# Choosing experts on ScalarE and VectorE: where the gate factors, the number lookup and the first-key rows are computed

## The chip, the core and the metric

One Trainium2 chip, one of its NeuronCores. The metric is the device time of one execution of the whole kernel, in microseconds (us); the number quoted for a kernel is the median of its runs. The engines are named as the profile names them: PE (TensorE, matrix products), DVE (VectorE), ACT (ScalarE), POOL (GpSimd) and SP (SyncE, which only issues transfers here). POOL also issues the gathers of expert rows.

## What is computed

One layer on 1024 tokens of 1024 values: a mixer of two groups (state space and convolution), then retrieval of experts, then a norm. The change lies in the retrieval. Cut to what matters:

```
s = einsum("thpd,hpkd->thpk", q, sub_keys)          # 8 heads, 2 halves, 128 keys each
sv, si = top_k(s, 16)                               # best 16 of 128 keys, both halves
cand = sv[:, :, 0, :, None] + sv[:, :, 1, None, :]
best, flat = top_k(cand.reshape(t, 8, 256), 16)     # best 16 of the pair sums
i1 = take(si[:, :, 0], flat // 16); i2 = take(si[:, :, 1], flat % 16)
experts = i1 * 128 + i2                             # 128 numbers out of 16384 for a token
gates = softmax(best)
act = gelu(einsum("pd,ped->pe", x, u_tab[experts]))
out = einsum("pe,ped->pd", gates * act, v_tab[experts])
```

## The kernel before, in words

Tokens come in eight blocks of 128 (z = 0 to 7). Blocks 0 to 4 are served densely: for every expert the product with all tokens is made, weighted by a gate matrix that is zero for experts that a token didn't choose. Blocks 5 to 7 are served by gathers: POOL issues indirect transfers of single expert rows, and DVE multiplies and adds them. Both kinds run side by side in the last stage (from about 1246 us to the end), where PE does the dense products.

Before that comes the stage of choice (some 717 to 1211 us). `select` (L1016) chooses the experts of a block. For each head DVE finds the best 16 of the 128 scores of each half (`top16`, L1024). POOL adds the pairs of key numbers (`stair` on POOL, L1056) and DVE adds the pairs of scores (L1057); then DVE finds the best 16 of 50 candidate sums. The number lookup follows: for each head, two one-hot arrays are made by comparison on DVE (L1081; 128x160 for the first eight places, 128x400 for the others), multiplied in place by the candidate numbers on POOL (L1083), and summed on DVE one head later (`place`, L1069). Then come the softmax (L1089 to L1097, its exponential on ACT) and the next block. `select` is a generator; each yield carries an estimated time.

For blocks 0 to 4, `gate_matrix` (L1166) writes the gate matrices to DRAM (`g_dram`). It takes four tokens (index t4) at a time, 32 times a block, 160 times in all:

- `second` (L1200): DVE compares the second key numbers with 0 to 127 and gets one-hot rows `ob` in bfloat16, laid out key by token (L1203). POOL multiplies them by the gates and writes `o2` token by key (L1205).
- `first` (L1208): one-hot rows `o1` of the first key number. Three times out of four DVE compares (L1211); the fourth time ACT computes relu(1 - |key - number|) in four activations of one token and one over all four (L1216, L1217).
- `outer` (L1186): PE multiplies `o2` by `o1` for each of the four tokens into one PSUM tile `pg` (L1189).
- `store` (L1192): ACT copies `pg` into a staging tile `stg` (L1196), laid out row, column, token. After every 16 of these SP writes the tile to `g_dram` (L1198).

One step of `gate_matrix` works on four groups at once: it stores group n-3, makes the second rows of n, the first rows of n-1 and the product of n-2 (L1222 to L1226). Buffers: 3 for `ob`, 4 for `o2`, 2 for `o1`, 3 for `pg`.

The order of work is written out: every engine carries out its instructions in the order in which the program issues them. While `select` runs for a block, `tick` (L1118) adds up the estimated times and issues one step of the waiting gate matrix for each 1.0 us, and one piece of the score products (L947, `scores`) for each 1.75 us. So the gate matrix of block z is woven into the choice for block z+1. At the end of the stage `prepare` (L994) makes the first dense products; it splits operands on DVE and POOL in turn (L1002, L61).

Block 7 is chosen inside the last stage: `choosing` (L1340) calls the same `select`, two heads at a time, and `advance` (L1347) issues one of its pieces after each group of dense products, and a step of `gathered` (L1272) where it is due. There POOL's queue holds both the lookup's products (L1083) with the sums of key numbers (L1035), and the gathers (L1281), in one order. A gather waits for one of five row buffers, which DVE frees by L1303 or L1315. PE's dense products use expert matrices that ACT and DVE split into a high and a low part (`lower_u`, L982; `hi_lo`, L61).

The places that the change touches:

Of the kernel before, what the change touches and what calls it, by code (L numbers as in the profile page):

```python
# [13 lines left out]
AF = mybir.ActivationFunctionType  # L14
OP = mybir.AluOpType
# [3 lines left out]
P = 128  # L19
# [53 lines left out]
def layer_kernel(ctx, tc, A, dbg=None):  # L73
    nc = tc.nc
# [10 lines left out]
    ones = glob.tile([P, P], F32, name="ones")  # L85
    nc.vector.memset(ones, 1.0)
    iot = glob.tile([P, P], F32, name="iot")
# [85 lines left out]
    with ExitStack() as st:  # L173
# [80 lines left out]
        for i in range(NZ):  # L254
            o = prb[:, i * P:(i + 1) * P] if i < NT else prc[:, (i - NT) * P:(i - NT + 1) * P]
# [111 lines left out]
    with ExitStack() as st:  # L367
# [126 lines left out]
        for n, c in enumerate(order):  # L494
# [5 lines left out]
            p, pc = project(n, 4 <= c < 10 or c == 20)  # L500
# [7 lines left out]
            elif c >= 16 and c < 20:  # L508
                i = c - 16
# [18 lines left out]
            else:  # L528
                i = c - 4
# [241 lines left out]
    with ExitStack() as st:  # L771
# [129 lines left out]
        for z in range(NT):  # L901
# [3 lines left out]
            p = multiply(z, 0, x1)  # L905
# [8 lines left out]
            p = multiply(z, 1, x1)  # L914
# [101 lines left out]
    def select(z, tp, nh, scores, put):  # L1016

        def together(chains):
            for c in zip(*chains):
                for f in c:  # L1020
                    f()
                yield len(c)
# [17 lines left out]
        for h0 in range(0, NH, nh):  # L1040

            v = tp.tile([P, nh, 2, TOPK], F32, name="v", bufs=1)
            ix = tp.tile([P, nh, 2, TOPK], U32, name="ix", bufs=1)
            for hh in range(nh // 2):
                s = scores(z, h0 // 2 + hh)
                for q in (0, 1):
                    for n in together([top16(v[:, 2 * hh + q, p], ix[:, 2 * hh + q, p], s[:, 2 * q + p],
                                             tp.tile([P, P], F32, name="scr", bufs=2)) for p in range(2)]):
                        yield 0.2 * n
            ixf = ix.bitcast(F32)  # L1050
            nc.vector.tensor_copy(ixf, ix)
            nc.vector.tensor_scalar(ixf[:, :, 0], ixf[:, :, 0], float(P), None, op0=OP.mult)
            yield 0.3

            cand = tp.tile([P, 2, nh, NCAND], F32, name="cand", bufs=1)
            stair(nc.gpsimd, ixf, cand[:, 1], UPPER + LOWER)  # L1056
            stair(nc.vector, v, cand[:, 0], SUMS)  # L1057
            yield 1.0
            best = tp.tile([P, nh, TOPK], F32, name="best", bufs=1)
            pos = tp.tile([P, nh, TOPK], U32, name="pos", bufs=1)  # L1060
            posf = tp.tile([P, nh, TOPK], F32, name="posf", bufs=1)
            ef, gt = put(z, h0)
            pend = []

            def place(n):
                while len(pend) > n:
                    q, oh = pend.pop(0)
                    for i, o in enumerate(oh):
                        nc.vector.tensor_reduce(ef[:, q, i * 8:i * 8 + 8], o, axis=mybir.AxisListType.X, op=OP.add)  # L1069

            for q2 in range(0, nh, 2):
                for n in together([top16(best[:, q], pos[:, q], cand[:, 0, q], tp.tile([P, NCAND], F32, name="c2", bufs=2))
                                   for q in (q2, q2 + 1)]):
                    yield 0.12 * n
                nc.vector.tensor_copy(posf[:, q2:q2 + 2], pos[:, q2:q2 + 2])
                for q in (q2, q2 + 1):
                    oh = tp.tile([P, 8, NUP + NCAND], F32, name="oh").rearrange("p a b -> p (a b)")
                    oh = [o.rearrange("p (a b) -> p a b", a=8) for o in (oh[:, :8 * NUP], oh[:, 8 * NUP:])]
                    for i, o in enumerate(oh):
                        sh = [P, 8, NCAND if i else NUP]  # L1080
                        nc.vector.tensor_tensor(o, posf[:, q, i * 8:i * 8 + 8, None].to_broadcast(sh),  # L1081
                                                lex[:, None, :sh[2]].to_broadcast(sh), op=OP.is_equal)
                        nc.gpsimd.tensor_tensor(o, o, cand[:, 1, q, None, :sh[2]].to_broadcast(sh), op=OP.mult)  # L1083
                    pend.append((q, oh))
                    yield 0.7
                    place(nh // 8)
                    yield 0.7
            eb = tp.tile([P, nh, TOPK], F32, name="eb", bufs=1)
            nc.vector.tensor_tensor(eb, best, best[:, :, 0:1].to_broadcast([P, nh, TOPK]), op=OP.subtract)  # L1089
            nc.scalar.activation(eb, eb, AF.Exp)  # L1090
            yield 0.2
            place(0)
            yield 0.9
            sm = tp.tile([P, nh], F32, name="sm")
            nc.vector.tensor_reduce(sm, eb, axis=mybir.AxisListType.X, op=OP.add)
            nc.vector.reciprocal(sm, sm)
            nc.vector.tensor_tensor(gt, eb, sm[:, :, None].to_broadcast([P, nh, TOPK]), op=OP.mult)  # L1097
            if z >= ND:
                nc.vector.tensor_copy(idx[:, z - ND, h0 * TOPK:(h0 + nh) * TOPK], ef.rearrange("p h k -> p (h k)"))
            yield 0.8  # L1100
# [5 lines left out]
    with ExitStack() as st:  # L1106
# [59 lines left out]
        def gate_matrix(z, ef, gt):  # L1166

            e2 = tp2.tile([P, 2, P], F32, name="e2", bufs=1)
            ei = e2[:, 0].bitcast(I32)
            nc.vector.tensor_copy(ei, ef)  # L1170
            nc.vector.tensor_scalar(ei, ei, P - 1, None, op0=OP.bitwise_and)
            nc.vector.tensor_copy(e2[:, 1], ei)
            nc.vector.tensor_tensor(e2[:, 0], ef, e2[:, 1], op=OP.subtract)
            nc.vector.tensor_scalar(e2[:, 0], e2[:, 0], 1.0 / P, None, op0=OP.mult)
            yield
            pt = psT.tile([P, 3, P], F32, name="pt")
            for j, src in enumerate((e2[:, 0], gt, e2[:, 1])):
                nc.tensor.transpose(pt[:, j], src, ident)
            tr = tp2.tile([P, 2, P], F32, name="tr", bufs=1)
            tb = tp2.tile([P, P], BF16, name="tb", bufs=1)  # L1180
            yield
            nc.scalar.activation(tr, pt[:, :2], AF.Copy)
            nc.scalar.activation(tb, pt[:, 2], AF.Copy)
            yield

            def outer(t4, o1, o2):  # L1186
                pg = psG.tile([P, 4, P], F32, name="pg")
                for j in range(4):
                    nc.tensor.matmul(pg[:, j], o2[:, j], o1[:, j], start=True, stop=True)  # L1189
                return t4, pg  # L1190

            def store(t4, pg):  # L1192
                if t4 % 16 == 0:
                    stg[0] = gst.tile([P, P, P // 2], F32, name="stg")
                o = t4 % 16 * 4
                nc.scalar.activation(stg[0][:, :, o:o + 4].rearrange("p i t -> p t i"), pg, AF.Copy)  # L1196
                if t4 % 16 == 15:
                    nc.sync.dma_start(g_dram[z, t4 // 16], stg[0])  # L1198

            def second(t4):  # L1200
                ts = slice(t4 * 4, t4 * 4 + 4)
                ob = tp2.tile([P, P, 4], BF16, name="ob", bufs=3)
                nc.vector.tensor_tensor(ob, iotx, tb[:, None, ts].to_broadcast([P, P, 4]), op=OP.is_equal)  # L1203
                o2 = tp2.tile([P, 4, P], F32, name="o2", bufs=4)
                nc.gpsimd.tensor_tensor(o2.rearrange("p t j -> p j t"), ob, tr[:, 1, None, ts].to_broadcast([P, P, 4]), op=OP.mult)  # L1205
                return t4, o2

            def first(t4, o2):  # L1208
                o1 = tp2.tile([P, 4, P], F32, name="o1")
                if t4 % 4 < 3:  # L1210
                    nc.vector.tensor_tensor(o1, iot[:, None].to_broadcast([P, 4, P]),  # L1211
                                            tr[:, 0, t4 * 4:t4 * 4 + 4, None].to_broadcast([P, 4, P]), op=OP.is_equal)
                else:
                    for j in range(4):
                        t = t4 * 4 + j
                        nc.scalar.activation(o1[:, j], iot, AF.Abs, bias=tr[:, 0, t:t + 1], scale=-1.0)  # L1216
                    nc.scalar.activation(o1, o1, AF.Relu, bias=ones[:, 0:1], scale=-1.0)  # L1217
                return t4, o1, o2

            stg = [None]  # L1220
            got = [None] * 3
            for t4 in range(P // 4 + 3):  # L1222
                if got[2]:
                    store(*got[2])
                got = [second(t4) if t4 < P // 4 else None, got[0] and first(*got[0]), got[1] and outer(*got[1])]
                yield  # L1226
# [369 lines left out]
```

## Time and profile before

| | |
|---|---|
| time, median of 3 runs | 3130.14 us (3124.53 to 3130.31) |
| the profiled execution's own time | 3129.54 us |
| its span in the profile | 3127.7 us |
| PE, DVE, POOL, ACT busy over the span | 91%, 84%, 55%, 32% |

The span is what the profiler sees between the first and the last instruction; the execution's own time has 1.84 us around it. Busy shares are means over the span; the stages differ, so the prediction goes by stretches. Matrix products on PE are pipelined, and their ends are modelled.

### The profile page before, as it was taken

How to read it: one execution, taken by the hardware profiler on the slowest of the kernel's cores; microseconds unless marked ns; L12 is line 12 of the kernel's file. 1: busy time of each engine (PE TensorE's matmuls, PEld its weight loads, DVE VectorE, ACT ScalarE, POOL GpSimd, SP SyncE). 2: the span in 40 equal slices, each digit the busy share in tenths (PEclk: the TensorE clock that was granted, in tenths of full speed). 3: DMA queues.
4: the chain of work that ended last, by engine and by line, in shares of the span. 5: the costliest groups of instructions: out<-in, count | busy, mean ns of one | idle time of the engine just before them, and what ended most of it. 6: DMA issues, size and time to landing. Idle time of an engine off the chain costs nothing.

```text
span 3127.7 us, 41600 instructions
## 1 busy us (share of the span) xinstructions
PE 2841.5 (91%) x14905; PEld 2381.7 (76%) x14905; DVE 2632.5 (84%) x4956; ACT 1011.7 (32%) x1584; POOL 1713.4 (55%) x1361
## 2 busy tenths in 40 slices
PE   7999777998888875999989999999999999999996
PEld 3777676764555555887878988998998898898885
DVE  5898788559999997889888888888888888888886
ACT  3224323333555652232222222222222322222222
POOL 0221454425676774666666666565566555556663
PEclk8999999999999887999999999999999999999998
DMA  6111355250222125888879999999998998999983
GB/s 209 61 40 42 112 150 184 81 188 7 115 108 108 55 122 199 286 277 314 297 273 326 320 336 339 328 334 326 327 334 315 328 349 314 334 335 322 327 290 127
DMA packets 334543, 722.65 MB, mean 231 GB/s; under 512 B 24560, under 2 KB 167168, under 8 KB 333056
## 3 DMA queue, kind: packets, MB, share of 16 engines
q0 software_dynamic: 112176, 408.47, 36.8%
q1 hardware_dynamic: 222160, 311.53, 29.0%
q8 instruction: 117, 1.92, 0.2%
q14 instruction: 90, 0.74, 0.1%
HBM read 658.56 MB, written 61.35 MB: 230 GB/s over the span
## 4 chain that ended last, share of the span: by engine, by line
PE 44%; DVE 29%; issue 10%; DMA 8%; POOL 6%; ACT 2%; SPq 0%; DVEq 0%; POOLq 0%; ACTq 0%
PE pa L990 18%; PE pv L1428 5%; PE pv L1429 5%; PE pv L1427 5%; POOL gr L1281 4%; DMA gr<-in_peer_u_dram,idx 4%; DVE cfm L408 3%; DVE o L1211 3%; PE pa L68 3%; DVE ob L1203 2%; PE pq L947 2%; DVE oh L1081 2%; DMA gr<-in_peer_v_dram,idx 2%; DVE gr L1303 1%; DVE h2T L1315 1%
## 5 line engine op out<-in xcount | busy, mean ns | idle before, releaser
L1281 POOL DMA_INDIRECT gr<-in_peer_v_dram,idx x384 | 537.6, 1400 | 325.5 <-DVE h2T L1315 219.1
L1281 POOL DMA_INDIRECT gr<-in_peer_u_dram,idx x384 | 523.8, 1364 | 347.9 <-DVE gr L1303 262.5
L1428 PE MATMUL pv<-vl,wh 128*128 128x512 f32 x1280 | 513.4, 401 | 26.0 <-DVE vl L61 25.9
L1315 DVE SCALAR_TENSOR_TENSOR h2T<-gr,wv,h2T 128x1024 f32<-128x1024 f32 x381 | 495.7, 1301 | 38.3 <-DMA gr<-in_peer_v_dram,idx 31.5
L1427 PE MATMUL pv<-vh,wl 128*128 128x512 f32 x1280 | 510.6, 399 | 7.2 <-ACT vh L60 7.0
L1303 DVE SCALAR_TENSOR_TENSOR gr<-gr,h2T 128x1024 f32<-128x1024 f32 x384 | 463.9, 1235 | 57.5 <-DMA gr<-in_peer_u_dram,idx 52.8
L1429 PE MATMUL pv<-vh,wh 128*128 128x512 f32 x1280 | 510.7, 399 | 0.0
L60 ACT ACTIVATE vh<-v 128x512 fp32r<-128x512 f32 x256 | 161.8, 632 | 682.6 <-PE pv L1429 656.1
L990 PE MATMUL pa<-hh,ul 128*128 128x320 f32 x2000 | 340.3, 313 | 40.1 <-DVE ul L982 39.2
L990 PE MATMUL pa<-hl,uh 128*128 128x320 f32 x2000 | 336.8, 311 | 8.3 <-ACT uh L978 8.3
L990 PEld LDWEIGHTS pa<-hh,ul 128*128 128x128 f32 x2000 | 306.6, 190 | 45.4 <-DVE ul L982 44.4
L990 PE MATMUL pa<-hh,uh 128*128 128x320 f32 x2000 | 337.6, 311 | 0.0
L990 PEld LDWEIGHTS pa<-hl,uh 128*128 128x128 f32 x2000 | 307.8, 190 | 11.3 <-ACT uh L978 8.6
L1428 PEld LDWEIGHTS pv<-vl,wh 128*128 128x128 f32 x1280 | 243.2, 190 | 92.4 <-DVE vl L61 35.7
L990 PEld LDWEIGHTS pa<-hh,uh 128*128 128x128 f32 x2000 | 307.5, 190 | 0.0
L1392 ACT ACTIVATE ga<-pa 128x320 f32<-128x320 f32 x252 | 110.0, 438 | 594.7 <-PE pa L990 571.0
L1427 PEld LDWEIGHTS pv<-vh,wl 128*128 128x128 f32 x1280 | 243.6, 190 | 66.4 <-ACT vh L60 8.2
L1429 PEld LDWEIGHTS pv<-vh,wh 128*128 128x128 f32 x1280 | 243.4, 190 | 57.8
L1205 POOL TENSOR_TENSOR o<-ob,tr 128x512 f32<-128x512 bf16 x160 | 216.5, 1355 | 110.7 <-DVE ob L1203 99.4
L1189 PEld LDWEIGHTS pg<-o,o 128*128 128x128 f32 x1280 | 173.9, 207 | 132.5 <-issue 66.4
L61 DVE TENSOR_TENSOR vl<-v,vh 128x512 fp32r<-128x512 f32 x256 | 184.4, 721 | 105.1 <-ACT vh L60 104.1
L1189 PE MATMUL pg<-o,o 128*128 128x128 f32 x1280 | 187.4, 297 | 78.8 <-DVE o L1211 53.9
(357 smaller groups left out, 4510.3 us busy)
## 6 DMA issues: line engine op xcount, KB each, us to landing
v<-in_peer_v_dram SPq DMA_DIRECT2D x256, 256.0 KB
u<-in_peer_ut_dram SPq DMA_DIRECT2D x87, 512.0 KB
g_dram<-stg SPq DMA_DIRECT2D x10, 4096.0 KB
gm<-g_dram SPq DMA_DIRECT2D x64, 640.0 KB
h2T<-in_peer_ut_dram SPq DMA_DIRECT2D x41, 512.0 KB
ld<-in_ada_w_dram SPq DMA_DIRECT2D x24, 512.0 KB
w<-in_w_in_t_dram SPq DMA_DIRECT2D x21, 512.0 KB
raw<-in_ada_w_dram SPq DMA_DIRECT2D x8, 1024.0 KB
```

The lines of the kernel that those rows point to most:

```text
L60: nc.scalar.activation(hi, src, AF.Copy)
L61: (eng or nc.vector).tensor_tensor(lo, src, hi.bitcast(F32), op=OP.subtract)
L990: nc.tensor.matmul(pa[half], x[:, k], y[:, k, half * TH:half * TH + TH], start=t == 0 and k == 0, stop=t == 2 and k == KD - 1)
L1189: nc.tensor.matmul(pg[:, j], o2[:, j], o1[:, j], start=True, stop=True)
L1205: nc.gpsimd.tensor_tensor(o2.rearrange("p t j -> p j t"), ob, tr[:, 1, None, ts].to_broadcast([P, P, 4]), op=OP.mult)
L1281: nc.gpsimd.indirect_dma_start(out=g, out_offset=None, in_=A[t], in_offset=bass.IndirectOffsetOnAxis(ap=idx[:, b, e:e + 1], axis=0))
L1303: nc.vector.scalar_tensor_tensor(g, g, 1.0, h2, op0=OP.mult, op1=OP.mult, accum_out=act[:, e:e + 1])
L1315: nc.vector.scalar_tensor_tensor(ac, g, wv[:, e:e + 1], ac, op0=OP.mult, op1=OP.add)
L1392: nc.scalar.activation(self.ga[:, half * TH:half * TH + TH], self.pa[half], AF.Gelu)
L1427: nc.tensor.matmul(Out.pv[t], wl[:, sl], self.vh, start=i == 0, stop=False)
L1428: nc.tensor.matmul(Out.pv[t], wh[:, sl], self.vl, start=False, stop=False)
L1429: nc.tensor.matmul(Out.pv[t], wh[:, sl], self.vh, start=False, stop=i == GE - 1)
```

## The change

Four edits in `select` and `gate_matrix`. The products of the number lookup move from POOL to DVE. The eviction of the gate matrix writes in the staging tile's own order (row, then four tokens in a run) and reads the PSUM tile in steps, where before it read PSUM in order and wrote in steps. The multiplication of the second-key rows by the gates becomes four activations with a scale per partition on ACT, in place of one operation on POOL. All first-key rows are made by comparison on DVE; the form on ACT is gone.

```diff
--- before.py
+++ after.py
@@ -1080,7 +1080,7 @@
                         sh = [P, 8, NCAND if i else NUP]
                         nc.vector.tensor_tensor(o, posf[:, q, i * 8:i * 8 + 8, None].to_broadcast(sh),
                                                 lex[:, None, :sh[2]].to_broadcast(sh), op=OP.is_equal)
-                        nc.gpsimd.tensor_tensor(o, o, cand[:, 1, q, None, :sh[2]].to_broadcast(sh), op=OP.mult)
+                        nc.vector.tensor_tensor(o, o, cand[:, 1, q, None, :sh[2]].to_broadcast(sh), op=OP.mult)
                     pend.append((q, oh))
                     yield 0.7
                     place(nh // 8)
@@ -1193,7 +1193,7 @@
                 if t4 % 16 == 0:
                     stg[0] = gst.tile([P, P, P // 2], F32, name="stg")
                 o = t4 % 16 * 4
-                nc.scalar.activation(stg[0][:, :, o:o + 4].rearrange("p i t -> p t i"), pg, AF.Copy)
+                nc.scalar.activation(stg[0][:, :, o:o + 4], pg.rearrange("p t i -> p i t"), AF.Copy)
                 if t4 % 16 == 15:
                     nc.sync.dma_start(g_dram[z, t4 // 16], stg[0])
 
@@ -1202,19 +1202,14 @@
                 ob = tp2.tile([P, P, 4], BF16, name="ob", bufs=3)
                 nc.vector.tensor_tensor(ob, iotx, tb[:, None, ts].to_broadcast([P, P, 4]), op=OP.is_equal)
                 o2 = tp2.tile([P, 4, P], F32, name="o2", bufs=4)
-                nc.gpsimd.tensor_tensor(o2.rearrange("p t j -> p j t"), ob, tr[:, 1, None, ts].to_broadcast([P, P, 4]), op=OP.mult)
+                for j in range(4):
+                    nc.scalar.activation(o2[:, j], ob[:, :, j], AF.Copy, scale=tr[:, 1, t4 * 4 + j:t4 * 4 + j + 1])
                 return t4, o2
 
             def first(t4, o2):
                 o1 = tp2.tile([P, 4, P], F32, name="o1")
-                if t4 % 4 < 3:
-                    nc.vector.tensor_tensor(o1, iot[:, None].to_broadcast([P, 4, P]),
-                                            tr[:, 0, t4 * 4:t4 * 4 + 4, None].to_broadcast([P, 4, P]), op=OP.is_equal)
-                else:
-                    for j in range(4):
-                        t = t4 * 4 + j
-                        nc.scalar.activation(o1[:, j], iot, AF.Abs, bias=tr[:, 0, t:t + 1], scale=-1.0)
-                    nc.scalar.activation(o1, o1, AF.Relu, bias=ones[:, 0:1], scale=-1.0)
+                nc.vector.tensor_tensor(o1, iot[:, None].to_broadcast([P, 4, P]),
+                                        tr[:, 0, t4 * 4:t4 * 4 + 4, None].to_broadcast([P, 4, P]), op=OP.is_equal)
                 return t4, o1, o2
 
             stg = [None]
```

## Rows read from the trace of the kernel before

**Rows 1.** Stretches; columns: us, busy PE, PEld, DVE, ACT, POOL, granted clock, DMA share, GB/s.
```profile
748.00:1180.00 432.00, 353.17 (x1682) 240.67 (x1681) 424.80 (x1624) 248.96 (x399) 307.14 (x306) 0.93 0.22 93
1246.00:1650.00 404.00, 367.86 (x1952) 329.14 (x1953) 344.00 (x708) 111.73 (x176) 255.56 (x217) 0.95 0.84 290
1650.00:2050.00 400.00, 395.48 (x2172) 353.82 (x2172) 346.99 (x437) 110.35 (x175) 246.56 (x178) 1.00 0.94 329
```

**Rows 2.** Waits from 748 to 1180 us: total us, times, longest.
```profile
ACT stg L1196 <- PE pg L1189: 138.4, 96, 5.2
...
PE pg L1189 <- DVE o L1211: 53.9, 38, 4.2
```

**Rows 3.** DVE's groups by shape, 717 to 1211 us: busy us, mean ns | idle before.
```profile
L1211 DVE TENSOR_TENSOR o<-iot,tr 128x512 f32<-128x512 f32 x120 | 100.0, 834 | 1.7 <-PE pg L1189 1.6
L1203 DVE TENSOR_TENSOR ob<-iotx,tb 128x512 bf16<-128x512 bf16 x160 | 95.6, 598 | 0.0
L1081 DVE TENSOR_TENSOR oh<-posf,lex 128x400 f32<-128x400 f32 x56 | 43.4, 775 | 0.0
...
L1081 DVE TENSOR_TENSOR oh<-posf,lex 128x160 f32<-128x160 f32 x56 | 23.1, 412 | 1.4
...
L1075 DVE CAST posf<-pos 128x32 f32<-128x32 uint32 x28 | 11.5, 410 | 0.8
```

**Rows 4.** The same lines one by one: shortest/median/longest ns, first and last start.
```profile
L1203 DVE TENSOR_TENSOR ob<-iotx,tb x160: 397/474/1258, 748.6 to 1173.7; 128x512 bf16<-128x512 bf16 x160
...
L1211 DVE TENSOR_TENSOR o<-iot,tr x120: 675/684/1551, 750.7 to 1174.0; 128x512 f32<-128x512 f32 x120
...
L1081 DVE TENSOR_TENSOR oh<-posf,lex x128: 309/562/1898, 721.3 to 1611.1; 128x160 f32<-128x160 f32 x64, 128x400 f32<-128x400 f32 x64
...
L1075 DVE CAST posf<-pos x32: 175/240/1082, 721.1 to 1596.8; 128x32 f32<-128x32 uint32 x32
```

**Rows 5.** Timeline, one meeting of POOL and DVE: start us, us.
```profile
885.48 1.54 POOL L1205 TENSOR_TENSOR o<-ob,tr 128x512 f32<-128x512 bf16 x1 [0.36 <-PE pg L1189]
...
885.98 1.26 DVE L1203 TENSOR_TENSOR ob<-iotx,tb 128x512 bf16<-128x512 bf16 x1
```

**Rows 6.** Timeline of DVE: two that depend, a step's start, two that don't depend.
```profile
744.34 0.23 DVE L1171 TENSOR_SCALAR e<-e 128x128 int32<-128x128 int32 x1
744.61 0.23 DVE L1172 CAST e<-e 128x128 f32<-128x128 int32 x1
...
758.16 0.41 DVE L1203 TENSOR_TENSOR ob<-iotx,tb 128x512 bf16<-128x512 bf16 x1
...
765.99 0.41 DVE L1203 TENSOR_TENSOR ob<-iotx,tb 128x512 bf16<-128x512 bf16 x1
766.32 0.68 DVE L1211 TENSOR_TENSOR o<-iot,tr 128x512 f32<-128x512 f32 x1
```

**Rows 7.** ACT: two groups by shape, then two merged pieces of its timeline.
```profile
L1196 ACT ACTIVATE stg<-pg 128x512 f32<-128x512 f32 x159 | 166.3, 1063 | 143.9 <-PE pg L1189 138.4 <-POOL o L1205 5.3
...
L953 ACT ACTIVATE s<-pq 128x512 f32<-128x512 f32 x24 | 14.9, 619 | 6.8 <-PE pq L947 6.8
...
882.26 1.24 ACT L1216 ACTIVATE o<-iot,tr 128x128 f32<-128x128 f32 x4
...
885.47 1.98 ACT L1196 ACTIVATE stg<-pg 128x512 f32<-128x512 f32 x2 [1.21 <-PE pg L1189]
```

**Rows 8.** 1246 to 1650 us: a wait's total, then timeline pieces of PE and POOL.
```profile
POOL oh L1083 <- DVE oh L1081: 30.2, 7, 9.6
...
1323.96 0.50 PE L1427 MATMUL pv<-vh,wl 128*128 128x512 f32 x1 [1.95 <-ACT vh L60]
...
1391.47 2.50 PE L990 MATMUL pa<-hh,ul 128*128 128x320 f32 x8 [5.52 <-DVE ul L982]
...
1611.36 2.60 POOL L1083 TENSOR_TENSOR oh<-oh,cand 128x160 f32<-128x160 f32 x2 [5.60 <-DVE oh L1081]
...
1621.43 2.50 PE L990 MATMUL pa<-hh,ul 128*128 128x320 f32 x8 [7.26 <-DVE ul L982]
```

## The prediction, made before the changed kernel was run

> **What bounds the kernel now.** I read the page's shares first, and they don't decide: PE and DVE are both busy most of the span. So I went by stretches, then by waits, then by DVE's groups and the single durations in them.
>
> In the stage of choice DVE is busy 424.8 of 432 us, PE 353, POOL 307, ACT 249 [rows 1]. A busy share of 98% on an engine that works in order means that its own work sets the pace. The waits agree: PE waits 53.9 us for DVE's first-key rows and ACT waits 138.4 us for PE [rows 2], while DVE's comparisons wait 1.6 us for PE in all [rows 3].
>
> But DVE's busy time isn't all work. The same comparison of one shape takes 0.40 us at best and 1.26 us at worst for `ob`, 0.68 (median) and 1.55 for `o1` [rows 4]; the means are 0.60 and 0.83 [rows 3]. One meeting shows why: POOL multiplies from 885.48 to 887.02, and an `ob` comparison that starts at 885.98 ends at 887.24, as if it had run its 0.40 us only once POOL was done [rows 5]. So POOL's two products (L1205, L1083) cost DVE time, though POOL itself is no bound.
>
> In the last stage PE sets the pace, with an exception. From 1650 to 2050 us it is busy 395.5 of 400 at a granted clock of 1.00; from 1246 to 1650, while block 7 is chosen, 367.9 of 404 at 0.95 [rows 1]: some 36 us idle against 4.5. There POOL waits 30.2 us for DVE's comparisons, seven times [rows 8], and while it waits its queue issues no gather. DVE, in order, then waits for the late row, the split matrix behind it comes late, and PE waits for that. Of PE's gaps over 1 us, seven (the first 1.95 us at 1324, the last 7.26 us at 1621) come up to some 10 us after a lookup product on POOL, 20.8 us in all; the others, as the 5.52 us before 1391, follow the sums of key numbers, which stay on POOL [rows 8].
>
> **The stage of choice, on DVE.** Seven blocks are chosen in it: 56 heads and 160 groups of four tokens.
>
> What leaves DVE is the waiting for POOL. From the groups' busy time [rows 3] I take the count times the undisturbed duration [rows 4]: `ob` 95.6 - 160 x 0.40 = 31.6; `o1` 100.0 - 120 x 0.684 = 17.9; the one-hots, 43.4 - 56 x 0.56 = 12.0 and 23.1 - 56 x 0.31 = 5.7; the casts of positions 11.5 - 28 x 0.18 = 6.5. That is 73.7 us. On POOL only the sums of key numbers and four splits are left. Bounds: none of it goes (0), or all of it and some 6 us more in small groups that I don't list (80). I take 77, nearer the upper end, since the undisturbed durations stand in the same trace.
>
> What comes to DVE, first: 112 lookup products. They aren't in DVE's trace; the nearest row is the comparison of the same shapes and type, 0.31 and 0.56 us [rows 4]. Each needs the result just before it. Dependent operations start 0.03 us after the end of the one in front, independent ones 0.08 before it (766.32 against 765.99 + 0.41) [rows 6]. So a head's four operations take 0.34 + 0.23 + 0.59 + 0.48 = 1.64 us where two take 0.23 + 0.48 = 0.71: 56 x 0.93 = 52 us more. Bounds: 40 us if they overlap like independent ones, 60 if the candidates' repeated rows read slower.
>
> Second: 40 first-key rows, 40 x (0.68 - 0.08) = 24 us.
>
> DVE's sum is 52 + 24 - 77 = -1, with -16 (40 + 24 - 80) as its lower end and +7 (60 + 24 - 77) as its upper; that POOL stays in the way is the last rival below.
>
> **New waits.** The exponential (L1090) now stands on ACT behind an eviction and four gate activations, and DVE's sum (L1095) is queued behind its result: seven times at most 2.1 us, 0 to 15 us. I take 1, since DVE has the last lookup sums and a step of the gate matrix in between. The lookup's products now wait on DVE for POOL's sums of key numbers; the search for the best 16 covers these, and in the last stage several pieces of dense work do; without that cover it is a POOL wait of the kind seen at 1391. `ob` has three buffers, now freed by ACT, which works behind PE: three steps of slack, no cost while ACT keeps up. SP's queue gets the same ten transfers. So the stage comes to 0.
>
> **ACT.** Per group of four it now does one eviction, 0.97 us from start to start (two in 1.98), and four activations, 1.24 us together and 1.15 behind one another, if they take what its four of the same shape take now [rows 7]; those are gone. With 0.1 for the scores' evictions (14.9 us [rows 7] over 160) that is 2.2 us a group. DVE has 425 us / 160 = 2.66 us a group in the mean, but less in quick stretches, beside the search among the 128 scores: four steps from 758.16 to 765.99, 1.96 each [rows 6], and 2.1 with their share (0.60/4) of the extra rows. By the estimated times in the code (16 of a block's 35 us) about half of the steps, 80, are such. So ACT is under DVE where an eviction takes less than some 0.87 us from start to start.
>
> The eviction's new price isn't in the trace. From PSUM to SBUF in order, 128x512 takes 0.62 us; written in steps of 256 bytes, 1.06 [rows 7]. It now writes runs of four and reads PSUM in steps of 512 bytes, which no row shows. Bounds: 0.62, and 1.50 if stepped reading costs 0.44 us too and none of the stepped writing's 0.44 goes. I take 0.7 (0.61 from start to start), nearer the first, since the step that made the known difference is gone. Then ACT costs nothing; it is DVE's work that hides it.
>
> [...]
>
> **The last stage.** POOL no longer waits for comparisons, so gathers go out earlier. At best the 20.8 us of PE's gaps go, and some of the time at the lower clock with them; at worst none goes, because the gathers find the next holdup. I take 16, since the stair sums and the full buffers stay. DVE gets 8 heads x 0.93 = 7.4 us more; it is busy 344 of 404 us there [rows 1], so its pauses hide most of it; I charge 2. Net -14, ends -21 and +7. PE after 1650 us is untouched.
>
> **Sum**, against the profiled execution's 3129.5 us: 0 - 14, or **3115.5 us**. The median of the runs, 3130.1, stands 0.6 us above that execution, so this is 0.47% below it. What a measurement of this kernel can tell from no change is about 0.2%, some 6 us.
>
> **Rivals.**
>
> *The gathers stay late.* The stair sums and the full buffers hold POOL as long as the products did, and the stage of choice breaks even: 3130 us, no difference. For it: PE's gaps behind stair sums, that of 5.52 us among them. Against: the longest, 7.26 us, follows a lookup product for which POOL had waited 5.60 us [rows 8]. Chance 0.21.
>
> *ACT becomes the bound*, the slower end. Place: the gate steps beside the search among 128 scores, 748 to 1180 us. It decides from an eviction of 0.87 us start to start. Price: with 0.97, as now, 80 x (2.2 - 2.1) = 8 us; with 1.40 (1.50 less the overlap), 80 x (2.65 - 2.1) = 44. I take the middle, 26: 3115.5 + 26 = 3141.5 us. For it: no row has the stepped reading. Against: only stepped writing has a price in rows. [...] Chance 0.20.
>
> *POOL wasn't what stretched DVE's operations*, so the relief doesn't come: 3115.5 + 77 = 3192.5 us. Against: the meeting [rows 5], and undisturbed durations in the same stage [rows 4]. Chance 0.03.
>
> **Numbers.** My forecast has 0.56; its own range is 3097 to 3125, from -12 to +8 in the stage of choice and -21 to -12 in the last. For 8 in 10 the range also takes in no difference and the nearer part of the ACT case: 3095 to 3146. Faster by over 0.2%: 0.53 of the forecast, 0.03 of the late gathers, 0.03 of the ACT case. Within 0.2%: 0.03, 0.16 and 0.06 of the same. Slower: 0.02 of the late gathers, 0.11 of the ACT case and the 0.03 of the last.
>
> **What would show it.** Right: `ob` near 0.40 us and `o1` near 0.68 in the mean, lookup products near 0.31 and 0.56 on DVE, the stage of choice still ending near 1211 us with DVE over 95% busy, evictions near 0.7, fewer and shorter PE gaps from 1246 to 1650. Wrong: DVE idle behind ACT, PE waiting for the gate activations, evictions over 0.96 us (0.87 from start to start), or the same PE gaps behind late gathers.

## The result

The changed kernel takes 3115.52 us (median of 5 runs, 3108.79 to 3116.64) against 3130.14 us before (median of 5, 3124.53 to 3139.56); the ratio is 0.9945, with a 95% interval of 0.9925 to 0.9965. The forecast was 3115.5 us.

Three stretches of the profile after, in the columns of [rows 1]:

```profile
748.00:1180.00 432.00, 350.58 (x1674) 238.94 (x1675) 420.63 (x1778) 302.22 (x843) 16.79 (x56) 0.92 0.22 93
1246.00:1650.00 404.00, 377.86 (x2061) 340.90 (x2062) 358.52 (x741) 117.73 (x186) 250.84 (x208) 0.96 0.88 304
1650.00:2050.00 400.00, 395.71 (x2135) 351.01 (x2134) 345.63 (x446) 107.59 (x171) 242.17 (x179) 1.00 0.94 331
```

In the stage of choice POOL has gone from 307 us of work to 17, ACT from 249 to 302, and DVE is as full as before: 421 of 432 us. From 1246 to 1650 us PE does 10 us more work in the same time; after 1650 nothing differs.

DVE's groups in the stage of choice after (717 to 1260 us), which answer to [rows 3]; L1083 is the lookup product, now on DVE:

```profile
L1211 DVE TENSOR_TENSOR o<-iot,tr 128x512 f32<-128x512 f32 x160 | 109.8, 686 | 0.2 <-PE pg L1189 0.2
L1203 DVE TENSOR_TENSOR ob<-iotx,tb 128x512 bf16<-128x512 bf16 x160 | 66.4, 415 | 0.0
L1083 DVE TENSOR_TENSOR oh<-oh,cand 128x400 f32<-128x400 f32 x56 | 32.2, 575 | 2.4
L1081 DVE TENSOR_TENSOR oh<-posf,lex 128x400 f32<-128x400 f32 x56 | 31.8, 569 | 0.1
...
L1081 DVE TENSOR_TENSOR oh<-posf,lex 128x160 f32<-128x160 f32 x56 | 19.4, 347 | 1.4
L1083 DVE TENSOR_TENSOR oh<-oh,cand 128x160 f32<-128x160 f32 x56 | 19.4, 346 | 2.4
...
L1075 DVE CAST posf<-pos 128x32 f32<-128x32 uint32 x28 | 5.9, 212 | 0.8
```

The means of the comparisons have come down to what was their undisturbed duration before: 0.415 from 0.598 us for `ob`, 0.686 from 0.834 for `o1`. The products cost what comparisons of their shapes do.

ACT's two new groups (L1206 is the gate multiplication), which answer to [rows 7], and the scores' eviction (L953), which reads PSUM and writes SBUF in order, for comparison:

```profile
L1206 ACT ACTIVATE o<-ob,tr 128x128 f32<-128x128 bf16 x640 | 209.4, 399 | 92.4 <-DVE ob L1203 90.4
L1196 ACT ACTIVATE stg<-pg 128x512 f32<-128x512 f32 x160 | 92.8, 580 | 16.4 <-PE pg L1189 16.3
L953 ACT ACTIVATE s<-pq 128x512 f32<-128x512 f32 x29 | 16.9, 583 | 25.6 <-PE pq L947 25.6
```

The eviction fell from 1.063 to 0.580 us, as fast as the one that does both in order (0.583).

**Where the time went.** Three events mark the stages in every kernel: the first score product (L947), the first product with a gathered row of the first table (L1303, after the change L1298), and the first multiply-add with one of the second table (L1315, then L1310). In the rows by line, the first of the two times is the first start. Before:

```profile
L947 PE MATMUL pq<-m,h2T x512: 592/592/1222, 681.0 to 1153.7; 128*128 128x512 f32 x171
...
L1303 DVE SCALAR_TENSOR_TENSOR gr<-gr,h2T x384: 1199/1218/2540, 1241.0 to 2753.8; 128x1024 f32<-128x1024 f32 x192
...
L1315 DVE SCALAR_TENSOR_TENSOR h2T<-gr,wv,h2T x381: 1265/1284/3433, 1569.7 to 3054.8; 128x1024 f32<-128x1024 f32 x191
```

After:

```profile
L947 PE MATMUL pq<-m,h2T x512: 592/592/1220, 686.1 to 1154.4; 128*128 128x512 f32 x171
...
L1298 DVE SCALAR_TENSOR_TENSOR gr<-gr,h2T x384: 1198/1221/1281, 1242.7 to 2739.1; 128x1024 f32<-128x1024 f32 x192
...
L1310 DVE SCALAR_TENSOR_TENSOR h2T<-gr,wv,h2T x381: 1267/1284/3436, 1556.6 to 3041.4; 128x1024 f32<-128x1024 f32 x191
```

The stage of choice, from the first to the second event, took 560.0 us and takes 556.6; the first table's part, in which most of block 7 is chosen, 328.7 and 313.9; the rest of the span 1558.0 and 1557.1. That is 19.1 us less. In the profiled execution after the change, the part ahead of the scores, which the change doesn't touch, came out 5.1 us longer, so the span shows 14.0. Such a later start (686 in place of 681 to 683 us) stands in two of the ten profiles below, so the stages are compared by their lengths:

| kernel | stage of choice | first table | rest | span | median | ratio to before (95%) |
|---|---|---|---|---|---|---|
| before | 560.0 | 328.7 | 1558.0 | 3127.7 | 3130.1 | |
| after | 556.6 | 313.9 | 1557.1 | 3113.7 | 3115.5 | 0.9945 (0.9925 to 0.9965) |
| e1: after, block 7's lookup on POOL | 556.1 | 323.1 | 1559.6 | 3120.9 | 3131.9 | 0.9982 (0.9968 to 0.9995) |
| e2: before, block 7's lookup on DVE | 559.4 | 314.1 | 1552.3 | 3107.2 | 3113.4 | 0.9937 (0.9912 to 0.9962) |
| e3: after, gates on POOL | 584.8 | 311.5 | 1560.6 | 3138.6 | 3141.1 | 1.0017 (1.0000 to 1.0034) |
| e4: after, eviction in steps | 557.9 | 314.0 | 1561.1 | 3120.0 | 3113.8 | 0.9925 (0.9902 to 0.9948) |
| e5: after, early lookup on POOL | 548.6 | 315.5 | 1557.7 | 3104.8 | 3106.3 | 0.9901 (0.9877 to 0.9925) |
| e6: after, block 7's sums on DVE | 555.5 | 303.4 | 1553.9 | 3094.0 | 3097.8 | 0.9885 (0.9863 to 0.9908) |
| e7: after, an eighth of the rows on ACT | 566.9 | 315.2 | 1557.2 | 3122.4 | 3127.5 | 0.9974 (0.9960 to 0.9988) |
| e8: e5 and e6 together | 547.3 | 303.6 | 1550.6 | 3084.0 | 3088.0 | 0.9856 (0.9829 to 0.9883) |

e1 to e4 ran on one chip and e5 to e8 on another; beside them the kernel before had medians of 3137.8 and 3135.9 us, so ratios say more than medians. Lengths are of one execution each. How far they scatter, kernels that are alike in a stage show: the stage of choice took 555.5 to 556.6 us in the changed kernel, e1 and e6, the first table's part 311.5 to 315.5 in the changed kernel, e2 to e5 and e7, and the rest 1550.6 to 1561.1 in all ten.

### The profile page after: what moved, and what is told of

Its sections match the earlier page's. It is cut to its first block, busy times and chain, and to the rows that moved or that the text cites. A ratio compares the mean times of both kernels' runs of the same rounds, so it can differ in the third digit from the quotient of the medians.

```text
span 3113.7 us, 41712 instructions
## 1 busy us (share of the span) xinstructions
PE 2838.8 (91%) x14905; PEld 2381.6 (76%) x14905; DVE 2624.8 (84%) x5124; ACT 1064.0 (34%) x2024; POOL 1386.1 (45%) x1073
## 4 chain that ended last, share of the span: by engine, by line
PE 43%; DVE 31%; issue 9%; DMA 8%; POOL 6%; ACT 2%; SPq 0%; DVEq 0%; POOLq 0%; ACTq 0%
PE pa L990 18%; PE pv L1423 5%; PE pv L1424 5%; PE pv L1422 5%; PE pa L68 4%; DMA gr<-in_peer_u_dram,idx 4%; POOL gr L1276 3%; DVE o L1211 3%; DVE gr L1298 2%; DVE cfm L408 2%; DMA gr<-in_peer_v_dram,idx 2%; DVE oh L1083 2%; DVE oh L1081 2%; DVE ob L1203 2%; DVE h2T L1310 2%
## 5 line engine op out<-in xcount | busy, mean ns | idle before, releaser
L1310 DVE SCALAR_TENSOR_TENSOR h2T<-gr,wv,h2T 128x1024 f32<-128x1024 f32 x381 | 494.8, 1299 | 38.4 <-DMA gr<-in_peer_v_dram,idx 32.0
L1298 DVE SCALAR_TENSOR_TENSOR gr<-gr,h2T 128x1024 f32<-128x1024 f32 x384 | 458.1, 1221 | 52.7 <-DMA gr<-in_peer_u_dram,idx 51.2
L1189 PE MATMUL pg<-o,o 128*128 128x128 f32 x1280 | 188.7, 298 | 73.0 <-ACT o L1206 62.3
L947 PE MATMUL pq<-m,h2T 128*128 128x512 f32 x512 | 242.9, 612 | 0.6 <-DMA m<-m_dram 0.6
```

The source lines that it names most:

```text
L947: nc.tensor.matmul(ps, h2T[:, k, z * P:(z + 1) * P], m[:, k, hh * 512:hh * 512 + 512], start=k == 0, stop=k == KD - 1)
L1298: nc.vector.scalar_tensor_tensor(g, g, 1.0, h2, op0=OP.mult, op1=OP.mult, accum_out=act[:, e:e + 1])
L1310: nc.vector.scalar_tensor_tensor(ac, g, wv[:, e:e + 1], ac, op0=OP.mult, op1=OP.add)
```

## The experiments

Two theories stood against each other. The queue theory: the gain lies in the last stage, because POOL's queue no longer waits for DVE's comparisons between its gathers; the stage of choice breaks even, since the products and rows that DVE takes over fill the time that POOL had made it wait. The stage theory: the gain comes from the stage of choice, and block 7 doesn't matter.

### e1: block 7's lookup products back on POOL

```diff
-                        nc.vector.tensor_tensor(o, o, cand[:, 1, q, None, :sh[2]].to_broadcast(sh), op=OP.mult)
+                        (nc.vector if z < NS else nc.gpsimd).tensor_tensor(o, o, cand[:, 1, q, None, :sh[2]].to_broadcast(sh), op=OP.mult)
```

> The changed kernel with the lookup products of block 7 alone back on POOL. Queue theory (the gain lies in the last stage, where POOL no longer waits for comparisons between its gathers): the gain of 14 us goes, 3126 to 3131 us, and the stretch from the first gathered product (L1303's successor, 1242.7 us) to the first product of the second table (1556.6 us) grows from 313.9 to about 328 us, as before. Stage theory (the gain comes from the stage of choice, block 7 doesn't matter): stays within 4 us of 3115.5, and that stretch stays near 314 us.

The first table's part grows from 313.9 to 323.1 us, short of the 328 expected; the stage of choice stays. By the ratios two thirds of the gain go ((0.9982 - 0.9945) / 0.0055), not all of it. The waits in that part (1238.2 to 1561.3 us; total, times, longest) show POOL standing before the lookup product again:

```profile
POOL oh L1083 <- DVE oh L1081: 21.5, 5, 9.7
```

### e2: that edit alone, in the kernel before

```diff
-                        nc.gpsimd.tensor_tensor(o, o, cand[:, 1, q, None, :sh[2]].to_broadcast(sh), op=OP.mult)
+                        (nc.gpsimd if z < NS else nc.vector).tensor_tensor(o, o, cand[:, 1, q, None, :sh[2]].to_broadcast(sh), op=OP.mult)
```

> The kernel before with the lookup products of block 7 alone moved to DVE, nothing else. Queue theory: the whole gain, 3114 to 3119 us, and about 314 us from the first gathered product to the first of the second table. Stage theory: no difference, 3127 to 3133 us, or slower by up to 7 us for the products that DVE gets in its last stage.

Close to the queue theory's numbers: 3113.4 us, just under its 3114 to 3119, and 314.1 us for the first table's part. Sixteen small products, moved to DVE, give what the whole change gives, within the intervals of the ratios. With e1 this settles where most of the gain lies. The first table's part before, after and in e2, in the columns of [rows 1]:

```profile
1241.00:1569.70 328.70, 300.35 (x1594) 268.10 (x1595) 284.73 (x628) 91.33 (x144) 207.45 (x176) 0.95 0.84 288
1242.70:1556.60 313.90, 295.17 (x1594) 264.85 (x1595) 282.80 (x640) 91.35 (x144) 192.71 (x162) 0.97 0.87 302
1240.80:1554.90 314.10, 294.67 (x1594) 264.16 (x1595) 282.74 (x640) 91.36 (x144) 189.47 (x163) 0.97 0.87 302
```

PE does the same 1594 products in 14.6 us less than before.

Why the products cost that time on POOL is less plain, for the queue isn't all of it. POOL's products also stretch DVE's multiplications by gathered rows where the two meet. One meeting before:

```profile
1306.46 2.66 POOL L1083 TENSOR_TENSOR oh<-oh,cand 128x160 f32<-128x160 f32 x2 [4.11 <-DVE oh L1081]
1308.22 1.99 DVE L1303 SCALAR_TENSOR_TENSOR gr<-gr,h2T 128x1024 f32<-128x1024 f32 x1
```

The median of that multiplication is 1.22 us. The 128 of them in this part took 158.0 us before, against 152.0 after, and all 384 of the run 463.9 us before and 463.8 in e1, against 458.1 after and 457.4 in e2; DVE's waits for gathered rows in this part were 21.3 and 19.5 us against 15.6 and 14.9. e1 and e2 move both effects at once, so they show the place of the gain and not the share of each. e6 tests the queue alone.

### e3: the gates on POOL

```diff
-                for j in range(4):
-                    nc.scalar.activation(o2[:, j], ob[:, :, j], AF.Copy, scale=tr[:, 1, t4 * 4 + j:t4 * 4 + j + 1])
+                nc.gpsimd.tensor_tensor(o2.rearrange("p t j -> p j t"), ob, tr[:, 1, None, ts].to_broadcast([P, P, 4]), op=OP.mult)
```

> The changed kernel with the multiplication by the gates back on POOL as one operation of four tokens. If POOL's operations are what stretches DVE's comparisons: the mean of the 160 second-key comparisons rises again from 0.415 to 0.5 us or more, that of the 160 first-key rows from 0.686 to 0.75 or more, and the stage of choice gets some 25 to 45 us longer (3140 to 3160 us). If something else stretched them: both stay at 0.42 and 0.69 and the time stays within 6 us of 3115.5.

The stage of choice is 28.2 us longer, as expected, and the whole by the ratios 0.72%, some 22 us. But the two comparisons hardly are longer: 0.449 and 0.697 us in the mean, where 0.5 and 0.75 or more were expected. The wait has moved to other operations. One meeting in the timeline:

```profile
888.71 1.40 POOL L1205 TENSOR_TENSOR o<-ob,tr 128x512 f32<-128x512 bf16 x1 [0.36 <-PE pg L1189]
889.09 1.16 DVE L1081 TENSOR_TENSOR oh<-posf,lex 128x160 f32<-128x160 f32 x1
```

POOL works until 890.11, and the one-hot comparison that started at 889.09 ends at 890.25. DVE's groups from 717 to 1236 us agree:

```profile
L1203 DVE TENSOR_TENSOR ob<-iotx,tb 128x512 bf16<-128x512 bf16 x160 | 71.9, 449 | 0.0
...
L1081 DVE TENSOR_TENSOR oh<-posf,lex 128x160 f32<-128x160 f32 x55 | 30.8, 560 | 1.3
...
L1075 DVE CAST posf<-pos 128x32 f32<-128x32 uint32 x28 | 11.2, 399 | 0.8
```

Against the changed kernel, the one-hots take 11.4 us more, the casts 5.3, `ob` 5.5: with `o1` (1.7) and the softmax's subtraction (4.5 against 2.0 us) some 26 us of waiting. So POOL's work does cost DVE time. Which operation pays seems to depend on which comes next when POOL starts; no run tests that by itself.

### e4: the eviction in steps again

```diff
-                nc.scalar.activation(stg[0][:, :, o:o + 4], pg.rearrange("p t i -> p i t"), AF.Copy)
+                nc.scalar.activation(stg[0][:, :, o:o + 4].rearrange("p i t -> p t i"), pg, AF.Copy)
```

> The changed kernel with the eviction writing in steps of 256 bytes, as before. If ACT still has room with evictions of 1.06 us: 3115 to 3119 us. If ACT then sets the pace in the quick stretches, as the slower rival has it: 80 x (2.2 - 2.1) = 8 us and more, with the true 0.30 us start to start of a gate activation nearer 15 us: 3123 to 3132, and DVE or PE waiting for ACT by several times what they do now (PE 62 us, DVE some 6 us).

No difference: 3113.8 us, ratio 0.9925 (its interval overlaps that of the change), and the stage of choice is 1.3 us longer. PE's waits for the gate activations are 54.6 us in the whole run, against 62.3 in the changed kernel. ACT's groups of this kernel:

```profile
L1206 ACT ACTIVATE o<-ob,tr 128x128 f32<-128x128 bf16 x640 | 206.9, 400 | 49.2 <-DVE ob L1203 49.0
L1196 ACT ACTIVATE stg<-pg 128x512 f32<-128x512 f32 x160 | 167.5, 1053 | 10.8 <-PE pg L1189 10.8
```

The eviction costs ACT 75 us more, and ACT still waits 49 us for DVE. That edit of the four shows no gain here, though it nearly halves its instruction.

### e5: the early lookup products on POOL

Blocks 0 to 6 on POOL, block 7 on DVE, the rest as changed.

```diff
-                        nc.vector.tensor_tensor(o, o, cand[:, 1, q, None, :sh[2]].to_broadcast(sh), op=OP.mult)
+                        (nc.gpsimd if z < NS else nc.vector).tensor_tensor(o, o, cand[:, 1, q, None, :sh[2]].to_broadcast(sh), op=OP.mult)
```

> The changed kernel with the lookup products of blocks 0 to 6 back on POOL; those of block 7 stay on DVE, the gates stay on ACT. DVE gives up 52 us of products and gets back what POOL's products make it wait. If the waits of POOL's two operations add up (77 us in the kernel before, 28 of them shown for the gate multiplication alone, so 49 for the lookup): 3112 to 3118 us, no difference to the changed kernel. If each alone costs less than its share, since nothing queues behind it (in block 0, where the lookup product was alone, the comparisons took 0.66 and 0.52 in place of 0.56 and 0.31 us, 17 us over 56 heads): 3085 to 3105 us.

The stage of choice is 8.0 us shorter, so the first forecast is out. The median, 3106.3 us, lies between the two; the ratio, 0.9901, which puts the kernel at some 3099 us beside 3130.1, lies in the second. DVE's groups from 717 to 1213 us:

```profile
L1211 DVE TENSOR_TENSOR o<-iot,tr 128x512 f32<-128x512 f32 x160 | 132.6, 829 | 1.4 <-PE pg L1189 1.4
...
L1203 DVE TENSOR_TENSOR ob<-iotx,tb 128x512 bf16<-128x512 bf16 x160 | 80.4, 502 | 0.0
...
L1081 DVE TENSOR_TENSOR oh<-posf,lex 128x400 f32<-128x400 f32 x56 | 35.9, 641 | 0.0
L1081 DVE TENSOR_TENSOR oh<-posf,lex 128x160 f32<-128x160 f32 x56 | 22.0, 393 | 1.4
```

DVE gives up 52 us of products and waits 22.8 + 14.0 + 4.1 + 2.6 = 43.5 us more: 8.5 us net, which the stage shows. So the lookup costs DVE some 44 us alone, the gates some 26; both together cost what the forecast took as 77, and of which 73.6 came (below). They nearly add.

### e6: block 7's sums of key numbers on DVE too

```diff
-            stair(nc.gpsimd, ixf, cand[:, 1], UPPER + LOWER)
+            stair(nc.gpsimd if z < NS else nc.vector, ixf, cand[:, 1], UPPER + LOWER)
```

> The changed kernel with the sums of block 7's key numbers moved to DVE too (eleven small additions for two heads, four times, some 5 us of DVE's time). Queue theory: PE's gaps behind them (1.95, 5.74, 1.51 and 6.62 us and some of the others) go: 3098 to 3108 us, and the stretch from the first gathered product of the first table to the first of the second falls from 314 to 300 to 307 us. Rival (the gathers are held by buffers and transfers, whatever POOL does): 3112 to 3121 us, the stretch 311 to 318 us.

This tests the queue theory where the change left POOL's queue as it was. In the changed kernel POOL waits for the key numbers, adds for 7.14 us (the four sets of sums take 3.34 to 7.27 us), and only then issues gathers; DVE runs out of rows. POOL's timeline, then DVE's:

```profile
1280.08 7.14 POOL L1035 TENSOR_TENSOR cand<-ix 128x16 f32<-128x16 f32 x11 [1.68 <-DVE ix L1052]
1287.37 1.81 POOL L1276 DMA_INDIRECT gr<-in_peer_u_dram,idx  x1
```

```profile
1292.45 1.22 DVE L1298 SCALAR_TENSOR_TENSOR gr<-gr,h2T 128x1024 f32<-128x1024 f32 x1 [4.09 <-DMA gr<-in_peer_u_dram,idx]
```

With the sums on DVE the first table's part falls to 303.4 us, 10.5 less, within the queue theory's 300 to 307, and the median is 3097.8 (ratio 0.9885). DVE's waits for gathered rows in that part, first in the changed kernel, then in this one:

```profile
DVE gr L1298 <- DMA gr<-in_peer_u_dram,idx: 15.6, 13, 4.5
```

```profile
DVE gr L1298 <- DMA gr<-in_peer_u_dram,idx: 3.1, 6, 1.2
```

Here the multiplications by gathered rows last what they did (median 1.222 us and at longest 1.270, against 1.221 and 1.281 in the changed kernel), so the 12.5 us that DVE saves here are waiting, not stretching.

### e7: an eighth of the first-key rows on ACT

```diff
-                nc.vector.tensor_tensor(o1, iot[:, None].to_broadcast([P, 4, P]),
-                                        tr[:, 0, t4 * 4:t4 * 4 + 4, None].to_broadcast([P, 4, P]), op=OP.is_equal)
+                if t4 % 8 < 7:
+                    nc.vector.tensor_tensor(o1, iot[:, None].to_broadcast([P, 4, P]),
+                                            tr[:, 0, t4 * 4:t4 * 4 + 4, None].to_broadcast([P, 4, P]), op=OP.is_equal)
+                else:
+                    for j in range(4):
+                        t = t4 * 4 + j
+                        nc.scalar.activation(o1[:, j], iot, AF.Abs, bias=tr[:, 0, t:t + 1], scale=-1.0)
+                    nc.scalar.activation(o1, o1, AF.Relu, bias=ones[:, 0:1], scale=-1.0)
```

> The changed kernel with every eighth group's first-key rows on ACT (absolute value and relu, as one in four before): DVE gives up 20 operations of 0.60 us, 12 us, and ACT gets 20 x 1.96 = 39 us. If DVE still sets the pace of the stage of choice: 3101 to 3106 us. If ACT is at its limit there already: 3113 us or more, and PE's waits for the gate activations (62 us) rise.

Slower than the changed kernel: ratio 0.9974 against 0.9945, the stage of choice 10.3 us longer, though DVE has 12 us less to do. Waits from 748 to 1180 us:

```profile
PE pg L1189 <- ACT o L1218: 36.7, 17, 4.8
PE pg L1189 <- ACT o L1206: 26.1, 22, 4.0
...
DVE o L1212 <- PE pg L1189: 18.2, 15, 2.7
```

PE's waits for ACT are in sum the 62 us of the changed kernel, but 36.7 of them are for the 20 first-key rows, which stand on ACT behind an eviction and four gate activations. PE passes the delay on to DVE, which waits 18.2 us (0.2 in the changed kernel) for one of the two `o1` buffers. ACT as a whole isn't full (329 of 432 us), so this looks like a matter of the order on it. Whether first-key rows ahead of the gates on ACT would pay was not tried.

### e8: e5 and e6 together

> The two edits of the early lookup on POOL and of block 7's sums on DVE together. They lie in different stages, so the differences to the changed kernel should add within 4 us, whatever each of them is: by the queue theory and lone waits 3075 to 3095 us; by added waits and a held gather 3111 to 3121 us.

The edits are the two diffs above: the early lookup products on POOL, block 7's products and sums on DVE, the gates on ACT. 3088.0 us, ratio 0.9856: faster than both kernels. The stage of choice takes 547.3 us (548.6 in e5), the first table's part 303.6 (303.4 in e6); the two gains stand side by side. By the ratios e5 and e6 lie 0.44% and 0.60% below the changed kernel and e8 0.89%; that is 0.15% short of the sum, less than the intervals (0.2% and more either way) can tell.

## Why the prediction was right

**DVE bounds the stage of choice, and POOL stretches its operations.** Right. The relief was taken as 77 us; the five groups that it was summed from give 29.2 + 17.8 + 11.6 + 3.7 + 5.6 = 67.9 of the 73.7 expected of them, and the softmax's subtraction and the cast of the key numbers 5.7 more, 73.6 in all. The products came as priced (0.575 and 0.346 us against 0.56 and 0.31), and so did the rows. The stage came out 3.4 us shorter where 0 was forecast, inside the ends of -12 and +8. e3 and e5, with one of POOL's two products each, show that it is POOL's work which DVE pays for.

**ACT stays under DVE.** Right, and more clearly than forecast: the eviction costs 0.58 us, not 0.7. The price put on the slower rival was wrong: it had ACT decide from 0.87 us between evictions and cost 8 us at the old price; e4 has that price, and its time isn't longer. The step that failed there compared the engines step by step in the quick stretches. Over the whole stage ACT had room; that the three `ob`, four `o2` and three `pg` buffers took up its lag is likely, but no run shows it. One sign that the prediction named for being wrong did appear, from 748 to 1180 us after:

```profile
PE pg L1189 <- ACT o L1206: 62.3, 52, 4.7
```

PE waits for the gate activations. It shows no cost: DVE, which sets the pace, waits 0.2 us for PE. What did cost time on ACT were first-key rows that PE soon needs (e7).

Writing in runs of four, in place of steps of 256 bytes, brought the eviction from 1.05 us (e4) to 0.58. The stepped reading of PSUM that came with it, priced at 0.44 us in the prediction's upper bound, didn't show: 0.580 us in steps of 512 bytes, 0.583 in order (L953).

**The last stage gives the gain.** Right in place and size: 14.8 us in the first table's part where 14 was forecast. Its make-up is another. By the busy columns in e2, 9.6 of the 14.8 us are idle time of PE (28.35 to 18.73) and 5.2 are busy time: the same 1594 products took less, at a mean granted clock of 0.97 in place of 0.95. The prediction put its 16 us down to the gaps and named the clock for the best case only. It also had DVE pay for the moved products and saw no relief there; they cost DVE 5.5 us in this part, and the multiplications that POOL no longer stretches give back 6.0. Three of PE's largest gaps after:

```profile
1388.11 2.50 PE L990 MATMUL pa<-hh,ul 128*128 128x320 f32 x8 [5.74 <-DVE ul L982]
...
1571.51 0.80 PE L1423 MATMUL pv<-vl,wh 128*128 128x512 f32 x1 [6.62 <-DVE vl L61]
...
1606.49 2.50 PE L990 MATMUL pa<-hh,ul 128*128 128x320 f32 x8 [4.08 <-DVE ul L982]
```

The first two follow the sums of key numbers, at much the same places as before (5.52 us before 1391 in [rows 8]); the gaps at 1324 and 1327 are gone, and that of 7.26 us at 1621 is now 4.08 at 1606. "The gathers stay late" was the rival for no difference; e1 and e2 exclude it. But half of its reason was true: the sums of key numbers did hold POOL, and moving them (e6) took another 10.5 us off.

**The sum was partly luck.** The forecast took 0 for the stage of choice and 14 for the last one. The stages give -19.1 us (-3.4, -14.8 and -0.9), the later start of that execution +5.1. By the lengths alone 3110.4 us would have been due; the interval of the ratio holds both.

## What to carry to other kernels

On a queue that issues transfers, look for the instructions that wait for another engine or are slow themselves (POOL's sums, 3.34 to 7.27 us): here they delayed the gathers behind them (DVE's waits for rows fell from 15.6 to 3.1 us with the sums on DVE), and moving sixteen small products off it (14.6 us in e2, part of it DVE's relief) was worth more than all that the change did in the stage of choice (3.4 us). An engine that is no bound can still be dear, if it slows the one that is; count what it costs there (44 us for the lookup, 26 for the gates) against what the bound would pay to do the work itself (52 us for the lookup), and decide for each stage apart, for the fastest kernel here has the same product on POOL in one stage and on DVE in the other.

## What the runs showed that was not expected

- With the gates alone on POOL (e3), some DVE operations took longer and others did not: the 128x160 comparison rose from 0.347 to 0.560 us and the cast from 0.212 to 0.399, while the sums (L1069) stayed at 0.31 and 0.56.
- ACT read PSUM in steps of 512 bytes as fast as in order (0.580 and 0.583 us for 128x512), while writing SBUF in steps of 256 bytes took 1.05 (e4).
- POOL's eleven small additions for two heads took 7.14 us beside the dense products. With the four sets on DVE (e6), DVE is busy 286.0 us in the first table's part against 282.8 in the changed kernel, from which some 0.8 us for eleven is an estimate. All the products of the lookup for two heads take DVE 2 x (0.575 + 0.346) = 1.8 us.
